# Latent scan of a gated DeltaNet: q products and intra-chunk products on the crossed quarters of the array

## The chip, the cores and the metric

The kernel runs on one core of a Trainium2 chip. The metric is the device time of one execution in microseconds (us). Three executions of the kernel before took 929.50, 930.94 and 931.32 us; their median is 930.94 us.

## The reference

One layer of a diffusion backbone: 512 latent tokens and 256 context tokens of width 1024. After modulation and RMSNorm one projection feeds two mixers, a windowed attention and a bidirectional gated DeltaNet; their outputs are projected, gated, summed, projected again and added to the stream, and an MLP follows. The change lies in the DeltaNet, which works in chunks of 64 tokens, for 8 heads of width 64 and two directions. A scan carries a 64 x 64 state per head from chunk to chunk:

```python
def step(S, xs):
    w_c, uv_c, qd_c, intra_c, kt_c, gl_c = xs
    u = uv_c - jnp.einsum('bhck,bhkv->bhcv', w_c, S)
    o = jnp.einsum('bhck,bhkv->bhcv', qd_c, S) + jnp.einsum('bhij,bhjv->bhiv', intra_c, u)
    S = jnp.exp(gl_c)[..., None, None] * S + jnp.einsum('bhck,bhcv->bhkv', kt_c, u)
    return S, o
```

The context scan (4 chunks) starts from zero and gives only its final states; these start the latent scans (8 chunks), forward and backward. The outputs of both directions are added, then normalized per head, scaled by `dn_norm_g` and multiplied by silu of a gate projection.

## The kernel before

Everything is in one program for one core. TensorE does the projections in three products each (high and low halves of both operands, in the fp32r type); the small products of the DeltaNet are plain float32. The compiler's planner orders each engine's instructions by its own estimates of when they are ready, and, among the ready ones, in the order in which the program writes them; it also places all semaphores. So the written order is a priority and not the order on the engine.

The heads lie in pairs: head pair q (0 to 3) has one head on partitions 0 to 63 and the other on 64 to 127. `r2` holds the two halves. A product on one half is a 64 x 64 product: its row half is where its two operands lie, its column half is where the result lies in PSUM.

`chain_step(d, step)` is one step of one direction, in three parts that are run in turn for both directions (`steps`). Part one multiplies the state with k and, in the latent scan, with q (L1116), and makes R from the k product on VectorE (L1120, L1121). Part two makes u (L1128), copies it scaled for the state (`uk`, VectorE, L1134) and plain for the output (`us`, ScalarE, L1138), and scales the q product into `zq` (ScalarE, L1140, one activation for each head pair, as the scale is one value per partition). Part three makes the next state: products of the k chunk with `uk` (L1147), the decayed old state (ScalarE, L1156), their difference (VectorE, L1158). Then the output: products of the intra-chunk matrices `IA` with `us` (L1165), added to `zq` (L1170); the direction that comes second to a chunk adds to the first one's result (L1173, L1175) and takes the sum of squares (L1176, L1177).

Each direction has two PSUM banks `zb[d]` for good: columns 0 to 255 hold the k products, 256 to 511 the q products, 512 to 767 u, 768 to 1023 the next state's products. The intra-chunk products get a bank of their own (`oi`).

Between the parts the loop at L1259 writes other work: `run_fill` with 8, 7 and 3 products of the gate projections (L1004, 128 x 128 by 512 columns), and `run_late`, which takes one piece of the late modulation (a 512 KB weight load, L1068, and a VectorE product with sum, L1070). The weights of the gate projections come through the same four buffers (L250) and are split into halves on ScalarE and VectorE (L259, L262). SP issues all loads.

After the scan the outputs are scaled (L1280), transposed (L1285) and multiplied by the gate's silu (L1290), where `a` picks the head of a pair.

Of the kernel before, what the change touches and what calls it, by code (L numbers as in the profile page):

```python
# [8 lines left out]
F32 = mybir.dt.float32  # L9
F32R = mybir.dt.float32r  # L10
BF16 = mybir.dt.bfloat16
AF = mybir.ActivationFunctionType
# [24 lines left out]
P = 128  # L37
# [5 lines left out]
HD = 64  # L43
NH = 8
CH = 64
# [54 lines left out]
def tile_layer(ctx: ExitStack, tc: tile.TileContext, I: dict, out: bass.AP, dbg=None):  # L100
    nc = tc.nc
    V, A, G, PE = nc.vector, nc.scalar, nc.gpsimd, nc.tensor
# [3 lines left out]
    const = ctx.enter_context(tc.tile_pool(name="const", bufs=1))  # L106
# [4 lines left out]
    def nm(s):  # L111
        uid[0] += 1
        return f"{s}_{uid[0]}"
# [5 lines left out]
    def small(shape, name, dt=F32, bufs=4, tag=None):  # L119
        return sb.tile(shape, dt, tag=tag or name, bufs=bufs, name=nm(name))  # L120

    alloc, bank = mem.get, lambda n=1: banks.get(n * 512)
# [60 lines left out]
    def split(src, hi, lo, eng=None):  # L183
        A.activation(r32(hi), src, AF.Copy)  # L184
        (eng or V).tensor_tensor(r32(lo), src, hi, op=ALU.subtract)  # L185
# [150 lines left out]
    for kt in range(KT):  # L336
        t = alloc(512)
        o = kt * 1024
# [316 lines left out]
    kT = [alloc(TOK, True) for _ in range(4)]  # L655
# [6 lines left out]
    t, t2 = alloc(TOK), alloc(TOK)  # L662
    ad, mx, be = t[0:32], t2[0:32], gb[32:64]
    for src, cols in ((abx, slice(0, SEQ)), (abc, slice(SEQ, TOK))):
        n = cols.stop - cols.start
# [27 lines left out]
    def col(c):  # L693

        return SEQ + c * CH if c < NCC else (c - NCC) * CH


    NM = NC_ * 4
# [16 lines left out]
    eG, tb, tbO = eg[:, 0:2], eg[:, 2:4], eg[:, 4]  # L715
# [180 lines left out]
    KTM, VTM = [None] * 3, [None] * 3  # L896
    qT = []
# [97 lines left out]
    szt, gdt = [], []  # L995
# [97 lines left out]
            next(fill, None)  # L1093


    oss = small([P, NCL, 4], "oss", bufs=1)
    hv = lambda ap: ap.rearrange("p (q v) -> p q v", q=4)
    state = [None, None]
# [3 lines left out]
    def chain_step(d, step):  # L1102
        lat = step >= NCC
        c = step if d == 0 else NC_ - 1 - (step - NCC) if lat else NCC - 1 - step
        cl = c - NCC if lat else c
        S, last = state[d], step == NC_ - 1
        m4 = slice(c * 4, c * 4 + 4)
        z = zb[d]
        r2 = [slice(0, 64), slice(64, 128)]
        vt = VTM[c // 4][:, c % 4 * 256:(c % 4 + 1) * 256]  # L1110

        if S is not None:
            for x, src in enumerate((kT, qT) if lat else (kT,)):
                for q in range(4):
                    for r in r2:
                        PE.matmul(z[r, x * 256 + q * HD:x * 256 + (q + 1) * HD], src[q][r, col(c):col(c) + CH],  # L1116
                                  S[r, q * HD:(q + 1) * HD], start=True, stop=True)
            Rb = alloc(256)
            R = Rb.ap
            V.tensor_tensor(hv(R), hv(z[:, 0:256]), bc(eG[:, d, m4], HD), op=ALU.mult)  # L1120
            V.scalar_tensor_tensor(R, vt, -0.5, R, op0=ALU.mult, op1=ALU.add)  # L1121
        else:
            R = vt
        yield
        u = z[:, 512:768]
        for q in range(4):
            for r in r2:
                PE.matmul(u[r, q * HD:(q + 1) * HD], XA[lat][d][r, (cl * 4 + q) * CH:(cl * 4 + q + 1) * CH],  # L1128
                          R[r, q * HD:(q + 1) * HD], start=True, stop=True)
        if S is not None:  # L1130
            Rb.free()
        if not last:
            uk = alloc(256)
            V.tensor_tensor(hv(uk.ap), hv(u), bc(tb[:, d, m4], HD), op=ALU.mult)  # L1134
        if lat:
            us, zqb = alloc(256), alloc(256)
            zq = zqb.ap
            A.activation(us.ap, u, AF.Copy)  # L1138
            for q in range(4):
                A.activation(zq[:, q * HD:(q + 1) * HD], z[:, 256 + q * HD:256 + (q + 1) * HD], AF.Copy,  # L1140
                             scale=eG[:, d, c * 4 + q:c * 4 + q + 1])
        yield
        if not last:
            sn = z[:, 768:1024]
            for q in range(4):
                for r in r2:
                    PE.matmul(sn[r, q * HD:(q + 1) * HD], KTM[c // 4][r, (c % 4 * 4 + q) * HD:(c % 4 * 4 + q + 1) * HD],  # L1147
                              uk[r, q * HD:(q + 1) * HD], start=True, stop=True)
            uk.free()
            Sn = Sb[d][step % 2]  # L1150
            if S is None:
                V.tensor_scalar(Sn.ap, sn, 0.5, None, op0=ALU.mult)
            else:
                se = alloc(256)
                for q in range(4):
                    A.activation(se[:, q * HD:(q + 1) * HD], S[:, q * HD:(q + 1) * HD], AF.Copy,  # L1156
                                 scale=egl[:, d, c * 4 + q:c * 4 + q + 1])
                V.tensor_tensor(Sn.ap, se.ap, sn, op=ALU.subtract)  # L1158
                se.free()
            state[d] = Sn  # L1160
        if lat:
            oi = bank()
            for q in range(4):
                for r in r2:
                    PE.matmul(oi[r, q * HD:(q + 1) * HD], IA[d][r, (cl * 4 + q) * CH:(cl * 4 + q + 1) * CH],  # L1165
                              us[r, q * HD:(q + 1) * HD], start=True, stop=True)
            us.free()
            dst = ot_[:, cl * 256:(cl + 1) * 256]
            if step - NCC < NCL // 2:
                V.tensor_tensor(dst, zq, oi[:, :256], op=ALU.add)  # L1170
                oi.free()
            else:
                V.tensor_tensor(zq, zq, oi[:, :256], op=ALU.add)  # L1173
                oi.free()
                V.tensor_tensor(dst, dst, zq, op=ALU.add)  # L1175
                A.activation(zq, dst, AF.Square)  # L1176
                V.tensor_reduce(oss[:, cl], hv(zq), axis=AX.X, op=ALU.add)  # L1177
            zqb.free()

    def steps(r):  # L1180
        for step in r:
            both = [chain_step(d, step) for d in range(2)]
            for _ in range(3):
                for g in both:
                    next(g, None)
                yield
# [42 lines left out]
    IA = [alloc(2048, True), alloc(2048, True)]  # L1229
# [39 lines left out]
    gdnh = small([P, 1], "gdnh", bufs=1)  # L1269
# [12 lines left out]
    for qq in range(2):  # L1282
        pt = bank(2)
        for c in range(NCL):
            PE.transpose(pt[:, c * P:(c + 1) * P], on[:, c * 256 + qq * P:c * 256 + (qq + 1) * P], ident)  # L1285
        for a in range(2):
            n = 2 * qq + a
            t = alloc(512)
            ct = lambda ap: ap.rearrange("p (c t) -> p c t", t=CH)
            V.scalar_tensor_tensor(ct(t.ap), pt.ap.rearrange("p (c a t) -> p c a t", a=2, t=CH)[:, :, a], gdnh, ct(szt[n].ap),  # L1290
                                   op0=ALU.mult, op1=ALU.mult)
            split(t.ap, yd[n][:, :512], yd[n][:, 512:])
            t.free()
            szt[n].free()
        pt.free()
# [106 lines left out]
    for hf in range(4):  # L1402
        act_ = []
        for f in range(FT):
# [7 lines left out]
            r, hl = alloc(1024), alloc(1024)  # L1412
# [135 lines left out]
```

## Time and profile before

| what | value |
|---|---|
| median of three runs | 930.94 us |
| profiled execution | 929.72 us |
| its span, first to last instruction | 927.7 us |
| granted TensorE clock, mean | 0.994 |
| TensorE busy | 894.8 us (96%) |
| VectorE busy | 597.7 us (64%) |
| ScalarE busy | 447.6 us (48%) |
| POOL busy | 12.1 us (1%) |
| latent scan, from its second k and q products to its last output products | 410.4 to 478.9 us |

The profile is one execution. PE is TensorE's products, PEld its weight loads, which overlap them, DVE VectorE, ACT ScalarE, POOL GpSimd, SP the queue that issues loads. A float32 product and its weight load stand in the trace as two records each. TensorE's products are pipelined and their ends are modelled, so their start times say more than their busy time. A row of a wait names who waited, for whom, how long in all, how often and how long at most. "m" stands for any buffer of the common arena, "banks" for PSUM.

### The profile page before, as it was taken

What the parts mean: (1) busy time and instruction counts of PE and PEld (TensorE: products, weight loads), DVE (VectorE), ACT (ScalarE), POOL (GpSimd) and SP (SyncE); (2) the same over time, 40 slices, a digit from 0 to 9 for tenths busy, and PEclk for the clock granted to TensorE, in tenths of its full rate; (3) what the DMA queues carried; (4) which work ended last, traced back from release to release, by engine and by line L of the source; (5) the groups of instructions that cost most, each with busy time, mean ns of one, the idle gap of its engine ahead of it and who ended that gap; (6) DMA issues with size and microseconds to landing.
All of it is one profiled execution on the core that took longest, in us unless ns stands there. A gap on an engine that the chain in (4) does not pass through costs nothing.

```text
span 927.7 us, 16848 instructions
## 1 busy us (share of the span) xinstructions
PE 894.8 (96%) x7082; PEld 721.1 (78%) x7082; DVE 597.7 (64%) x1021; ACT 447.6 (48%) x827; POOL 12.1 (1%) x26
## 2 busy tenths in 40 slices
PE   8999998999899999899999999999999999999998
PEld 5668767867677687778878879988888888888886
DVE  3587898997787997458756977971555235424511
ACT  5577753267568786565554434560243025213400
POOL 0000000000000002000000000000000000000000
PEclk9999998999999999999999999999999999999999
DMA  9650112210001232335424673680444224222111
GB/s 356 260 186 1 47 47 68 57 51 17 17 13 35 61 101 93 93 111 169 134 72 146 193 236 127 181 273 23 155 121 133 56 74 144 93 70 88 46 46 45
DMA packets 28443, 98.24 MB, mean 106 GB/s; under 512 B 3536, under 2 KB 4176, under 8 KB 27344
## 3 DMA queue, kind: packets, MB, share of 16 engines
q1 hardware_dynamic: 28368, 97.18, 32.7%
q8 instruction: 55, 0.90, 0.4%
q14 instruction: 20, 0.16, 0.1%
HBM read 95.07 MB, written 2.10 MB: 105 GB/s over the span
## 4 chain that ended last, share of the span: by engine, by line
PE 77%; DVE 11%; ACT 6%; DMA 3%; issue 2%; SPq 0%; DVEq 0%; ACTq 0%
PE banks L313 17%; PE banks L315 16%; PE banks L314 16%; PE banks L1004 10%; PE banks L1049 2%; PE banks L1116 2%; DVE wl L262 2%; PE banks L571 1%; PE banks L1147 1%; DMA wa<-in_wada 1%; PE banks L1128 1%; PE banks L577 1%; PE banks L639 1%; DVE m L834 1%; DVE m L833 1%
## 5 line engine op out<-in xcount | busy, mean ns | idle before, releaser
L313 PE MATMUL banks<-m,m 128*128 128x512 f32 (+1 forms) x600 | 223.3, 377 | 2.7 <-DVE m L620 1.9
L314 PE MATMUL banks<-m,m 128*128 128x512 f32 (+1 forms) x600 | 224.6, 376 | 0.1
L315 PE MATMUL banks<-m,m 128*128 128x512 f32 (+1 forms) x600 | 224.4, 376 | 0.0
L259 ACT ACTIVATE m<-wr 128x1024 fp32r<-128x1024 f32 x68 | 71.9, 1058 | 159.0 <-PE banks L314 80.4
L313 PEld LDWEIGHTS banks<-m,m 128*128 128x128 f32 x600 | 111.8, 188 | 25.8 <-ACT m L319 2.5
L314 PEld LDWEIGHTS banks<-m,m 128*128 128x128 f32 x600 | 112.5, 188 | 22.0 <-DVE m L320 1.5
L262 DVE TENSOR_TENSOR m<-wr,m 128x1024 fp32r<-128x1024 f32 x68 | 83.1, 1224 | 71.7 <-ACT m L259 35.4
L315 PEld LDWEIGHTS banks<-m,m 128*128 128x128 f32 x600 | 112.5, 188 | 21.4 <-issue 1.2
L1004 PE MATMUL banks<-m,wh 128*128 128x512 f32 x320 | 103.6, 400 | 3.0 <-ACT m L148 1.9
L315 PE MATMUL banks<-m,wl 128*128 128x512 f32 (+1 forms) x280 | 101.6, 365 | 4.7 <-DVE wl L262 4.7
L313 PE MATMUL banks<-m,wh 128*128 128x512 f32 (+1 forms) x280 | 104.0, 372 | 1.8 <-DVE m L595 1.0
L314 PE MATMUL banks<-m,wh 128*128 128x512 f32 (+1 forms) x280 | 102.8, 367 | 0.0
L1432 DVE SCALAR_TENSOR_TENSOR m<-banks,modT,m 128x512 f32<-128x512 f32 x32 | 24.0, 750 | 101.0 <-PE banks L315 101.0
L262 DVE TENSOR_TENSOR wl<-wr,wh 128x1024 fp32r<-128x1024 f32 (+1 forms) x58 | 62.1, 1071 | 28.6 <-ACT wh L259 28.5
L259 ACT ACTIVATE wh<-wr 128x1024 fp32r<-128x1024 f32 (+1 forms) x58 | 54.5, 940 | 41.7 <-PE banks L314 18.8
L1004 PEld LDWEIGHTS banks<-m,wh 128*128 128x128 f32 x320 | 58.9, 188 | 15.6 <-ACT m L148 2.2
L1004 PE MATMUL banks<-m,wl 128*128 128x512 f32 x160 | 64.7, 404 | 0.0
L315 PEld LDWEIGHTS banks<-m,wl 128*128 128x128 f32 x280 | 54.2, 195 | 12.8 <-DVE wl L262 5.4
L313 PEld LDWEIGHTS banks<-m,wh 128*128 128x128 f32 x280 | 54.4, 194 | 10.2 <-DVE m L595 1.3
L184 ACT ACTIVATE m<-m 128x512 fp32r<-128x512 f32 (+1 forms) x56 | 35.2, 631 | 54.5 <-DVE m L1415 21.3
L314 PEld LDWEIGHTS banks<-m,wh 128*128 128x128 f32 x280 | 54.4, 194 | 7.6 <-issue 1.0
L185 DVE TENSOR_TENSOR m<-m,m 128x512 fp32r<-128x512 f32 (+1 forms) x56 | 38.3, 688 | 18.8 <-ACT m L184 18.3
(236 smaller groups left out, 1279.2 us busy)
## 6 DMA issues: line engine op xcount, KB each, us to landing
wr<-in_wm SPq DMA_DIRECT2D x64, 512.0 KB, 3.7
wr<-in_win SPq DMA_DIRECT2D x38, 512.0 KB, 3.6
wa<-in_wada SPq DMA_DIRECT2D x32, 512.0 KB, 3.8
m<-in_wada SPq DMA_DIRECT2D x8, 1024.0 KB, 12.8
m<-in_xT SPq DMA_DIRECT2D x8, 512.0 KB, 5.7
wr<-in_wbr SPq DMA_DIRECT2D x16, 256.0 KB, 2.6
wr<-in_wout SPq DMA_DIRECT2D x8, 512.0 KB, 4.4
out<-m SPq DMA_DIRECT2D x8, 256.0 KB, 2.0
```

Source lines behind the costliest of these rows:

```text
L184: A.activation(r32(hi), src, AF.Copy)
L185: (eng or V).tensor_tensor(r32(lo), src, hi, op=ALU.subtract)
L259: h = A.activation(r32(hi), raw, AF.Copy)
L262: V.tensor_tensor(r32(lo), raw, hi, op=ALU.subtract)
L313: PE.matmul(acc, w[0][:, k, :], xhi, start=(start and i == 0), stop=False)
L314: PE.matmul(acc, w[0][:, k, :], xlo, start=False, stop=False)
L315: PE.matmul(acc, w[1][:, k, :], xhi, start=False, stop=(stop and i == n - 1))
L571: PE.transpose(pt[:, j * P:(j + 1) * P], probs[j][:, i * P:(i + 1) * P], ident)
L1004: PE.matmul(acc.ap, w[x][:, k, :], hx[k][y], start=(k == p == 0), stop=(k == KT - 1 and p == 2))
L1049: PE.matmul(pa.ap, w[x][:, j, :], r32(Q[y][:, :, j, :]), start=(j == p == 0), stop=(j == 3 and p == 2))
L1116: PE.matmul(z[r, x * 256 + q * HD:x * 256 + (q + 1) * HD], src[q][r, col(c):col(c) + CH], S[r, q * HD:(q + 1) * HD], start=True, stop=True)
L1432: V.scalar_tensor_tensor(xn_[ct], acc.ap, modT[:, 3, ct:ct + 1], xn_[ct], op0=ALU.mult, op1=ALU.add)
```

## The change

In the latent scan the q products are written to the other half of the partitions: the head on partitions 0 to 63 gets its q product on 64 to 127 and the other way round. The same holds for the intra-chunk products, so that both still meet in the sum; the output then holds the two heads of each pair exchanged, and the last hunk takes `1 - a` for `a`. The q products are written in turn with the k products, head pair by head pair, and the intra-chunk products in turn with those of the next state. In the banks of a direction q moves to columns 512 to 767 and u to 256 to 511, so k and u share one bank, and q and the next state's products the other. The scale of `zq` needs its halves exchanged too: `eGs` is a copy of `eG` with the halves swapped, made once by two ScalarE copies before the scans. The bank `oi` is taken before the next state's products instead of after them.

```diff
+    eGs = const.tile([P, 2, NM], F32, name="eGs")
+    for r in range(2):
+        A.activation(eGs[64 * r:64 * r + 64], eG[64 * (1 - r):64 * (1 - r) + 64], AF.Copy)
...
-            for x, src in enumerate((kT, qT) if lat else (kT,)):
-                for q in range(4):
-                    for r in r2:
-                        PE.matmul(z[r, x * 256 + q * HD:x * 256 + (q + 1) * HD], src[q][r, col(c):col(c) + CH],
+            for q in range(4):
+                for x, src in enumerate((kT, qT) if lat else (kT,)):
+                    for i, r in enumerate(r2):
+                        PE.matmul(z[r2[i ^ x], x * 512 + q * HD:x * 512 + (q + 1) * HD], src[q][r, col(c):col(c) + CH],
                                   S[r, q * HD:(q + 1) * HD], start=True, stop=True)
...
-        u = z[:, 512:768]
+        u = z[:, 256:512]
...
-                A.activation(zq[:, q * HD:(q + 1) * HD], z[:, 256 + q * HD:256 + (q + 1) * HD], AF.Copy,
-                             scale=eG[:, d, c * 4 + q:c * 4 + q + 1])
+                A.activation(zq[:, q * HD:(q + 1) * HD], z[:, 512 + q * HD:512 + (q + 1) * HD], AF.Copy,
+                             scale=eGs[:, d, c * 4 + q:c * 4 + q + 1])
         yield
+        sn = z[:, 768:1024]
+        oi = bank() if lat else None
+        for q in range(4):
+            o = slice(q * HD, (q + 1) * HD)
+            for r in r2:
+                if not last:
+                    PE.matmul(sn[r, o], KTM[c // 4][r, (c % 4 * 4 + q) * HD:(c % 4 * 4 + q + 1) * HD],
+                              uk[r, o], start=True, stop=True)
+            for i, r in enumerate(r2):
+                if lat:
+                    PE.matmul(oi[r2[1 - i], o], IA[d][r, (cl * 4 + q) * CH:(cl * 4 + q + 1) * CH],
+                              us[r, o], start=True, stop=True)
         if not last:
-            sn = z[:, 768:1024]
-            for q in range(4):
-                for r in r2:
-                    PE.matmul(sn[r, q * HD:(q + 1) * HD], KTM[c // 4][r, (c % 4 * 4 + q) * HD:(c % 4 * 4 + q + 1) * HD],
-                              uk[r, q * HD:(q + 1) * HD], start=True, stop=True)
             uk.free()
...
         if lat:
-            oi = bank()
-            for q in range(4):
-                for r in r2:
-                    PE.matmul(oi[r, q * HD:(q + 1) * HD], IA[d][r, (cl * 4 + q) * CH:(cl * 4 + q + 1) * CH],
-                              us[r, q * HD:(q + 1) * HD], start=True, stop=True)
             us.free()
...
-            V.scalar_tensor_tensor(ct(t.ap), pt.ap.rearrange("p (c a t) -> p c a t", a=2, t=CH)[:, :, a], gdnh, ct(szt[n].ap),
+            V.scalar_tensor_tensor(ct(t.ap), pt.ap.rearrange("p (c a t) -> p c a t", a=2, t=CH)[:, :, 1 - a], gdnh, ct(szt[n].ap),
```

## The prediction

> **What bounds the kernel now.** I read the head of the page first, then the table of stretches over the latent scan, then the chain that ended last, then the waits.
>
> ```profile
> span 927.7 us, 16848 instructions
> PE 894.8 (96%) x7082; PEld 721.1 (78%) x7082; DVE 597.7 (64%) x1021; ACT 447.6 (48%) x827; POOL 12.1 (1%) x26
> ```
>
> TensorE is busy for 96% of the span, but its ends are modelled, so this alone proves nothing about one stage. The changed lines run in the latent scan, whose steps 1 to 7 I cut at the start of their k and q products (columns: stretch, its length, then busy us with instruction counts of PE, PEld, DVE, ACT and POOL, granted clock, DMA share, GB/s):
>
> ```profile
> 410.40:420.30 9.90, 9.90 (x181) 8.09 (x182) 7.31 (x15) 5.51 (x23) 0.00 (x0) 1.00 0.35 108
> 420.30:430.10 9.80, 9.80 (x179) 7.97 (x179) 7.87 (x18) 4.69 (x16) 0.00 (x0) 1.00 0.56 163
> 430.10:440.90 10.80, 10.37 (x181) 8.27 (x180) 9.56 (x21) 6.72 (x24) 0.00 (x0) 1.00 0.72 209
> 440.90:450.80 9.90, 9.90 (x181) 8.09 (x182) 7.69 (x20) 6.30 (x22) 0.00 (x0) 1.00 0.66 201
> 450.80:460.70 9.90, 9.90 (x181) 8.07 (x183) 8.13 (x20) 4.31 (x16) 0.00 (x0) 1.00 0.36 100
> 460.70:470.50 9.80, 9.80 (x180) 7.97 (x180) 6.72 (x16) 6.13 (x21) 0.00 (x0) 1.00 0.19 66
> 470.50:478.90 8.40, 8.40 (x145) 6.73 (x144) 4.99 (x17) 4.67 (x14) 0.00 (x0) 1.00 0.31 96
> ```
>
> A step takes 9.8 to 9.9 us, all of it TensorE; only the step at 430 is longer. VectorE is next with 6.7 to 9.6 us. The chain through one step (start, length, work, instructions) is TensorE without a break:
>
> ```profile
> 440.93 2.01 PE banks L1116 x64
> 442.94 2.04 PE banks L1004 x8
> 444.98 1.08 PE banks L1128 x32
> 446.06 1.81 PE banks L1004 x7
> 447.88 0.61 PE banks L1147 x16
> 448.49 0.47 PE banks L1165 x16
> 448.95 0.47 PE banks L1147 x16
> 449.42 0.47 PE banks L1165 x16
> 449.89 0.90 PE banks L1004 x3
> ```
>
> A float32 product stands as two records, so 64 records at L1116 are the 32 products of both directions. TensorE itself waited twice in the whole scan, 1.5 us in all:
>
> ```profile
> PE banks L1004 <- ACT wh L259: 1.1, 1, 1.1
> PE banks L1147 <- ACT m L1138: 0.4, 1, 0.4
> ```
>
> So here the sum of the TensorE pieces is the time, and what shortens L1116, L1147 and L1165 shortens the step, until VectorE is in the way.
>
> **The change part by part: the products.** Before, the two products of one head pair use two quarters of the array (lower rows to lower columns, upper to upper). L1165 has 16 records in 0.47 us: eight pairs, 59 ns a pair. After, four products that use four different quarters stand next to each other. No row of before has the two crossed quarters together with the straight ones, so I bound the price of a group of four. The nearest rows are these (start, length, operation, shape, count):
>
> ```profile
> 76.51 1.57 PE L704 MATMUL banks<-c_prm,m 64*64 64x16 f32 x48
> 381.74 1.10 PE L754 MATMUL banks<-m,m 64*32 64x64 f32 x64 [0.19 <-ACT m L148]
> L704 PE MATMUL banks<-c_prm,m 64*64 64x16 f32 x48 | 1.6, 207 | 0.0
> L754 PE MATMUL banks<-m,m 64*32 64x64 f32 x256 | 4.2, 217 | 0.2 <-ACT m L148 0.2
> ```
>
> L704 has the same 64 rows feed both column halves, one product after the other: (1.57 - 0.21) / 24 = 57 ns a pair, though only 16 columns stream, so it is the loading of the 64 weight columns that takes this time, and two loads from one row half pass at once. L754 has each row half feed two column groups, with 64 columns streaming: (1.10 - 0.22) / 16 = 55 ns for four records, not for two. So one row half can feed two places at once, in weights and in data, and four records can run in the time of two. Not shown is that two row halves write the same column half at once, and both loads at full width in all four quarters. The ends: 59 ns for four (all overlap) and 118 ns for four (they take turns, no gain). I take 59, since L754 is the nearest: same streaming length, same number of records in flight.
>
> Per stage 32 pairs become 16 groups, 16 x 0.059 = 0.94 us less: L1116 from 2.01 to 1.07, the four rows of L1147 and L1165 from 2.02 to 1.08. L1128 stays. The latent scan has eight k and q stages and seven with both L1147 and L1165 (the last step has no next state). The first k and q stage isn't on the path; the planner has put it ahead, at 388 to 392 us, where the path is ScalarE's copies of the intra-chunk matrices:
>
> ```profile
> 398.80 0.63 ACT m L1249
> 399.66 1.33 ACT m L1140 x6
> 401.99 5.99 PE banks L1004 x25
> ```
>
> So 14 stages count: 14 x 0.94 = 13.2 us off TensorE's path.
>
> By the Trainium skill, page TensorE: Matmul & The Clock Gate, Part 3, The mechanism, a weight load runs under a product in flight only where the row group differs. By that rule the crossed pair, which shares its rows with the straight one, would load behind it, and the saving would be near zero. The trace doesn't agree so far: at L754 two tiles share each row half and still four records pass in 55 ns.
>
> **VectorE takes part of it back.** In the seven stretches VectorE's busy time is 7.31 + 7.87 + 9.56 + 7.69 + 8.13 + 6.72 + 4.99 = 52.3 of 68.5 us, and the change removes none of it. Its two longest waits are these (total, times, longest):
>
> ```profile
> DVE m L1158 <- PE banks L1147: 5.2, 4, 2.1
> DVE m L1070 <- DMA wa<-in_wada: 3.5, 4, 1.2
> ```
>
> The wait on TensorE shrinks with it; the 3.5 us on weights for the late modulation don't. VectorE takes its queue in order, so what waits behind L1070 are L1120, L1121, L1134 and L1158, and TensorE waits for these. I put the longer of the two engines for each stretch. TensorE: the stretch less 1.88 (the last less 0.94). VectorE: its busy time plus its DMA waits where the timeline has them:
>
> ```profile
> 428.05 1.23 DVE L1070 SCALAR_TENSOR_TENSOR m<-wa,m 128x1024 f32<-128x1024 f32 x1 [1.15 <-DMA wa<-in_wada]
> 435.76 1.22 DVE L1070 SCALAR_TENSOR_TENSOR m<-wa,m 128x1024 f32<-128x1024 f32 x1 [1.20 <-DMA wa<-in_wada]
> 445.53 1.23 DVE L1070 SCALAR_TENSOR_TENSOR m<-wa,m 128x1024 f32<-128x1024 f32 x1 [0.78 <-DMA wa<-in_wada]
> ```
>
> That gives 8.02; 7.87 + 1.15 = 9.02; 9.56 + 1.20 = 10.76; 7.69 + 0.78 = 8.47; 8.13; 7.92; 7.46. The sum is 59.8, where TensorE alone needs 68.5 - 13 x 0.94 = 56.3. So 3.5 us are lost again, nearly all in the steps at 420 and 430, where L1070 is dense. The bounds: 0 (VectorE works ahead in the lighter steps) and 7 (the same again for stalls inside a step, where a product waits for L1121 or L1138 while the step as a whole has room).
>
> **Waits that move.** Two waits of before are between readers and writers of different columns of the same PSUM bank:
>
> ```profile
> ACT m L1140 <- DVE m L1120: 7.3, 6, 2.1
> PEld banks L1147 <- ACT m L1138: 2.0, 4, 0.9
> 444.39 0.93 ACT L1140 ACTIVATE m<-banks,eg 128x64 f32<-128x64 f32 x4 [0.88 <-DVE m L1120]
> ```
>
> L1140 needs nothing from L1120, and L1147 nothing from L1138; what they share is the bank, so the program orders accesses by bank. After, k and u share one bank, q and the next state the other. L1140 no longer waits for L1120, which is worth nothing, as ScalarE isn't the path. The next state's products now wait for L1140 (through the bank) where they waited for L1138, and behind them in TensorE's queue stand the fill products L1004 and the next step's L1116. In the step shown, the second L1140 ends at 445.3 and L1147 starts at 447.8: 2.5 us of cover, of which TensorE's shorter first stage takes 0.94. Cost 0; without that cover 0.93 us for four scalings a direction. The products with us (L1165) now stand between the state's own, so the state waits for L1138 too, as it already did through the bank.
>
> **Small parts.** The two added copies for the swapped scales run once before the scans, 64 x 96 elements each. Between these rows,
>
> ```profile
> L1156 ACT ACTIVATE m<-m,egl 128x64 f32<-128x64 f32 x44 | 11.7, 339 | 5.8 <-DVE m L1158 5.7
> L1247 ACT ACTIVATE m<-m 32x512 f32<-32x512 f32 x1 | 0.6, 630 | 0.0
> ```
>
> one takes 0.34 to 0.63 us, two at most 0.8 by the nearer row with its extra columns. Their source is ready long before, so they fit into ScalarE's earlier gaps: 0, or 0.8 if they fall where ScalarE sets the path. The swapped half at L1290 and the other scale tile cost nothing: same operations, counts and shapes. No DMA is added or moved, and SP's and POOL's queues are as before.
>
> **Sum.** 13.2 - 3.5 - about 0.3 for the copies and lost order = 9.4 us. Against the profiled execution, 929.72 us (span 927.7 and 2.0 around it), that is 920.3; the median of the three runs, 930.94, is 1.2 above it, so 921.5.
>
> **The rivals.**
> 1. The whole saving arrives. For it: VectorE's longest wait is on TensorE, and the planner may set L1070 elsewhere. Against: the DMA waits. 930.94 - 13.2 = 917.7; chance 0.13.
> 2. The planner takes state and output products apart. One step of before shows that it does this where it thinks the copy of u late:
>
> ```profile
> 437.80 0.68 PE L1147 MATMUL banks<-m,m 64*64 64x64 f32 x16 [0.43 <-ACT m L1138]
> 438.84 0.68 PE L1147 MATMUL banks<-m,m 64*64 64x64 f32 x16
> 439.36 1.15 PE L1165 MATMUL banks<-m,m 64*64 64x64 f32 x32
> ```
>
> Both L1147 run ahead of both L1165. Were it so in every step, only the seven k and q stages gain: 6.6, less 1 for VectorE: 925.3. Chance 0.14, with VectorE at the far end of its bounds.
> 3. The change doesn't do what it says: the crossed products take turns with the straight ones, 118 ns for four. L1116 to L1165 keep their times: 930.9. Against it is L754; for it, that no row shows two row halves on one column half. Chance 0.08.
> 4. Slower: where two row halves write the same columns, the array has to empty between them. An emptying has a price in the chain above: L1147 after L1004 takes 0.61, L1165 right after L1147 0.47, so 0.14 a change. With a change between straight and crossed pairs, 16 in a direction's stage, 32 in a stage: 14 x 32 x 0.14 = 63 us, so 994. It decides as soon as a change costs anything over the zero of rival 3. Neither L704 nor L754 shows a pause between tiles of one row half. Chance 0.07, in which I count unlikelier ways of the same sign.
>
> **How the numbers follow.** My forecast, 918.5 to 924.5, has 0.58; rival 1 has 0.13, rival 2 0.14, rival 3 0.08, rival 4 0.07. A measurement of this kernel can tell about 0.2%, 1.9 us. Faster: 0.58 + 0.13 + 0.14 = 0.85; same 0.08; slower 0.07. The range goes from 916.5 (rival 1 with 1.2 us less, as the profiled run lies below the median) to 927 (past rival 2, with VectorE's 7 us): it leaves out rivals 3 and 4.
>
> **What would show it.** Right: 64 records of the k and q stage in about 1.1 us, the mixed stage of both directions in 1.1, steps of 8 to 8.5 us, VectorE over 85% busy in them, and new TensorE waits on L1121, L1138 or L1158 around the dense L1070. Wrong in the products: the stage still at 2.0 us. Wrong in the cover: TensorE waiting for L1140. The forecast fails low if the steps at 420 and 430 shrink like the others, and high if state products run alone.

## The result

| kernel | median, us | executions | ratio to the kernel before, 95% interval |
|---|---|---|---|
| before | 931.15 | 20 | |
| after | 926.64 (923.26 to 929.45) | 20 | 0.9953 [0.9939, 0.9966] |

The kernel is 4.5 us faster where 9.4 us were forecast. The time lies in the forecast's range and the sign is right, but less than half of the gain came: the forecast was wrong in its size. The step that failed is the term for VectorE. The profiled execution of after took 923.26 us, 6.5 less than that of before, and is the quickest of its twenty; the difference between single executions is taken up at the end.

The head of the page of after, the two lines that answer to the first two of before:

```profile
span 921.5 us, 16859 instructions
PE 886.7 (96%) x7082; PEld 709.2 (77%) x7082; DVE 596.6 (65%) x1021; ACT 447.6 (49%) x829; POOL 12.0 (1%) x26
```

VectorE and ScalarE have the work they had; ScalarE's two new instructions are the copies for the swapped scales. The timeline of TensorE in after (start, length, line, shape, count of records) shows the k and q products, then the first and last rows of a mixed stage:

```profile
410.68 1.16 PE L1119 MATMUL banks<-m,m 64*64 64x64 f32 x64
411.77 0.50 PE L1004 MATMUL banks<-m,wl 128*128 128x512 f32 x1
...
425.24 0.27 PE L1152 MATMUL banks<-m,m 64*64 64x64 f32 x2
425.29 0.27 PE L1156 MATMUL banks<-m,m 64*64 64x64 f32 x2
...
426.37 0.50 PE L1004 MATMUL banks<-m,wl 128*128 128x512 f32 x1
```

(L1119 was L1116, L1152 was L1147, L1156 was L1165.) The k and q products take 411.77 - 410.68 = 1.09 us to the next instruction, where 1.07 was forecast and 2.01 stood before. The mixed stage takes 426.37 - 425.24 = 1.13. Now the steps, cut as for before at the start of their k and q products (length, then busy us of PE, PEld, DVE, ACT and POOL, clock, DMA share, GB/s):

```profile
410.70:418.80 8.10, 8.10 (x183) 6.21 (x182) 6.49 (x16) 4.64 (x19) 0.00 (x0) 1.00 0.45 134
418.80:427.70 8.90, 8.44 (x183) 6.35 (x182) 7.99 (x17) 5.14 (x19) 0.00 (x0) 1.00 0.62 180
427.70:438.20 10.50, 9.41 (x178) 6.98 (x178) 9.81 (x24) 6.63 (x24) 0.00 (x0) 1.00 0.73 208
438.20:446.70 8.50, 8.50 (x180) 6.47 (x179) 7.14 (x17) 5.10 (x20) 0.00 (x0) 1.00 0.66 215
446.70:455.90 9.20, 8.11 (x181) 6.21 (x180) 7.83 (x19) 4.88 (x19) 0.00 (x0) 1.00 0.28 92
455.90:465.40 9.50, 8.47 (x179) 6.49 (x178) 6.91 (x17) 6.44 (x22) 0.00 (x0) 1.00 0.35 106
465.40:473.30 7.90, 7.24 (x143) 5.73 (x143) 6.41 (x16) 4.78 (x14) 0.00 (x0) 1.00 0.37 102
sum 62.60, PE 58.27 PEld 44.43 DVE 52.58 ACT 37.61 POOL 0.00; mean PE 8.32 PEld 6.35 DVE 7.51 ACT 5.37 POOL 0.00
```

| step | 1 | 2 | 3 | 4 | 5 | 6 | 7 | sum |
|---|---|---|---|---|---|---|---|---|
| forecast | 8.02 | 9.02 | 10.76 | 8.47 | 8.13 | 7.92 | 7.46 | 59.8 |
| after | 8.1 | 8.9 | 10.5 | 8.5 | 9.2 | 9.5 | 7.9 | 62.6 |

Step 7 is cut here, and in all sums over a scan below, where its last output product starts; that of before was cut where it ends, so the 68.5 us of before are 0.2 us longer by their cut. In this execution steps 1 to 4 go as forecast, to 0.3 us. Steps 5 to 7 take 26.6 instead of 23.5 us, and in none of them is an engine busy all the time: at step 6 TensorE has 8.47 of 9.5 us and VectorE 6.91. TensorE's longest waits over this scan (us in all, times, longest):

```profile
PE banks L1131 <- DVE m L1124: 1.9, 2, 1.1
PE banks L1119 <- DVE m L1168: 1.0, 2, 0.7
PE banks L1152 <- DVE m L1137: 0.9, 1, 0.9
```

Each is a small VectorE operation of the recurrence. Step 5 shows why it is late. VectorE's timeline there, and the product that waits:

```profile
448.04 0.68 DVE L626 SCALAR_TENSOR_TENSOR m<-m,banks 128x512 f32<-128x512 f32 x1
448.64 1.22 DVE L262 TENSOR_TENSOR wl<-wr,wh 128x1024 fp32r<-128x1024 f32 x1
449.78 0.41 DVE L1182 TENSOR_REDUCE oss<-m 128x4 f32<-128x256 f32 x1
450.11 0.74 DVE L1123 TENSOR_TENSOR m<-banks,eg 128x256 f32<-128x256 f32 x2
450.77 0.75 DVE L1124 SCALAR_TENSOR_TENSOR m<-m,m 128x256 f32<-128x256 f32 x2
...
451.24 1.15 PE L1131 MATMUL banks<-m,m 64*64 64x64 f32 x32 [1.09 <-DVE m L1124]
```

The k products started at 446.7 and were done about 1.1 us later. VectorE then still had the gate's output L626, the split of the fill weights L262 and a sum of squares (L1182) ahead of L1123. From 448.0 us on it works without a pause: nothing was missing for these, they only stood first in its queue. Between this stage and u the program writes eight fill products, 2.04 us in the chain of before. Before, the stage itself took 2.01 us, so VectorE had 0.94 us more to come through its queue. The same step of before shows that it needed nearly all of it:

```profile
451.79 1.22 DVE L262 TENSOR_TENSOR wl<-wr,wh 128x1024 fp32r<-128x1024 f32 x1
453.92 0.75 DVE L1121 SCALAR_TENSOR_TENSOR m<-m,m 128x256 f32<-128x256 f32 x2
454.77 1.15 PE L1128 MATMUL banks<-m,m 64*64 64x64 f32 x32
```

The queue is the same, L626 and L262 ahead of L1120 and L1121 (L1123 and L1124 of after). L1121 ends at 453.92 + 0.75 = 454.67, and L1128 starts at 454.77: 0.1 us to spare, where the change takes 0.94 away. In step 6 of after the same thing happens a part later, behind ScalarE:

```profile
460.61 1.23 DVE L262 TENSOR_TENSOR wl<-wr,wh 128x1024 fp32r<-128x1024 f32 x1 [1.28 <-ACT wh L259]
461.76 0.68 DVE L626 SCALAR_TENSOR_TENSOR m<-m,banks 128x512 f32<-128x512 f32 x1
462.35 0.74 DVE L1137 TENSOR_TENSOR m<-banks,eg 128x256 f32<-128x256 f32 x2
...
462.92 0.41 PE L1152 MATMUL banks<-m,m 64*64 64x64 f32 x6 [0.91 <-DVE m L1137]
```

VectorE stands idle for 1.28 us at L262 until ScalarE has made the high half, and L1137, which the next state needs, stands behind it.

### The profile page after: what moved, and what is told of

It reads as the page before. It is cut to its first block, busy times and chain, and to the rows that moved or that the text cites. A ratio compares the mean times of both kernels' runs of the same rounds, so it can differ in the third digit from the quotient of the medians.

```text
span 921.5 us, 16859 instructions
## 1 busy us (share of the span) xinstructions
PE 886.7 (96%) x7082; PEld 709.2 (77%) x7082; DVE 596.6 (65%) x1021; ACT 447.6 (49%) x829; POOL 12.0 (1%) x26
## 4 chain that ended last, share of the span: by engine, by line
PE 45%; DVE 3%; DMA 3%; ACT 1%; issue 1%; ACTq 0%
PE banks L313 14%; PE banks L314 14%; PE banks L315 14%; PE banks L1004 3%; DMA wa<-in_wada 2%; DVE m L1070 1%; DVE wl L262 1%; DMA wr<-in_wm 0%; ACT wh L259 0%; DVE m L1168 0%; ACT m L1166 0%; PE banks L1131 0%; PE banks L1290 0%; PE banks L1156 0%; ACT m L148 0%
## 5 line engine op out<-in xcount | busy, mean ns | idle before, releaser
L262 DVE TENSOR_TENSOR m<-wr,m 128x1024 fp32r<-128x1024 f32 x68 | 83.1, 1224 | 69.9 <-PE banks L314 34.2
L262 DVE TENSOR_TENSOR wl<-wr,wh 128x1024 fp32r<-128x1024 f32 (+1 forms) x58 | 62.1, 1071 | 29.7 <-ACT wh L259 29.3
```

Source lines behind the costliest of these rows:

```text
L262: V.tensor_tensor(r32(lo), raw, hi, op=ALU.subtract)
```

## The experiments

All times are medians, and the kernels are told in the order in which they ran, four at a time; before, run beside them, had 930.31, 931.5, 930.97 and 930.39 us for the four groups. "Scan" is the sum of the seven steps, as in the table above. The theory at the start was the forecast's: TensorE's saving is whole, and VectorE, held by the late modulation, takes part of it back.

**One part of the change at a time.** The first kernel keeps the crossed quarters and writes the products in the old order:

```diff
-            for q in range(4):
-                for x, src in enumerate((kT, qT) if lat else (kT,)):
+            for x, src in enumerate((kT, qT) if lat else (kT,)):
+                for q in range(4):
...
+        if lat:
+            oi = bank()
+            for q in range(4):
+                o = slice(q * HD, (q + 1) * HD)
+                for i, r in enumerate(r2):
+                    PE.matmul(oi[r2[1 - i], o], IA[d][r, (cl * 4 + q) * CH:(cl * 4 + q + 1) * CH],
+                              us[r, o], start=True, stop=True)
```

> The changed kernel with its crossed quarters, its bank layout and its scale copy, but with the products in the old order: all k, then all q; all of the next state, then the intra-chunk ones. Theory A (the gain comes from four quarters at once, and the rest of the change costs nothing): k and q stage 2.0 us again, state and output stage 2.0, time of the kernel before within 1 us. Rival B (the new bank layout or the new plan costs something by itself): 1 to 4 us slower than before, with waits on L1143 or a worse order in the scan.

928.71 us, 0.9987 [0.9975, 0.9999], scan 67.6. The stage did not go back to 2.0 us. TensorE's timeline of this kernel, where the program now has all L1151 of a direction ahead of its L1171:

```profile
413.00 1.56 PE L1119 MATMUL banks<-m,m 64*64 64x64 f32 x64
414.49 0.50 PE L1004 MATMUL banks<-m,wl 128*128 128x512 f32 x1
...
419.45 0.51 PE L1151 MATMUL banks<-m,m 64*64 64x64 f32 x10
419.75 0.27 PE L1171 MATMUL banks<-m,m 64*64 64x64 f32 x2
419.79 0.28 PE L1151 MATMUL banks<-m,m 64*64 64x64 f32 x3
```

The stage takes 414.49 - 413.00 = 1.49 us, between the 1.09 of the written turns and the 2.01 of before. Of the 16 records of the first direction's L1151 only ten have started when L1171, written behind all of them, starts on the other two quarters. The planner didn't mix them: in TensorE's instructions as this kernel compiles, the 16 records of L1151 stand together and the 16 of L1171 behind them. So TensorE starts products ahead of their order when their quarter is free, but only a little ahead; writing them in turn gives the other 0.4 us. The Trainium skill, page TensorE: Matmul & The Clock Gate, Part 3, The mechanism, says that products start and end in strict order; for the starts, these rows do not agree.

The next two kernels put the old order back in one of the two places only (the k and q products in turn; the mixed stage in turn).

> Only the k and q products in turn; next state first and then intra-chunk as before. TensorE loses 7 x 0.92 = 6.4 us in the scan. Theory A (VectorE's queue takes back what goes past its own need): 3 to 5 us faster than before, so most of what the whole change gave (4.3 us). Rival C (each stage's saving arrives in the same share, about a third): 2 us faster.

> Only the next state's and the intra-chunk products in turn; k first and then q. TensorE loses 7 x 0.92 = 6.4 us. Theory A: 3 to 5 us faster than before. Rival C: 2 us faster. The two halves of the change adding to more than the whole (4.3 us) speaks for A, to just the whole for C.

927.62, 0.9969 [0.9957, 0.9981], scan 65.3, and 925.74, 0.9959 [0.9942, 0.9976], scan 63.9. Both stages have their sizes where nothing holds them up, 1.09 in turn and 1.49 not, so against the old order the k and q stages give 7 x 0.4 = 2.8 us on TensorE and the mixed ones 6 x 0.4 = 2.4. The old order itself takes 13 x 0.52 = 6.8 us off TensorE against before, and its scan is only 0.9 us shorter: something else has become the limit. Whether the savings of the two halves add up can't be told. They gain 930.31 - 927.62 = 2.7 and 930.31 - 925.74 = 4.6 us over before, the old order 1.6 and the whole change 4.5, with intervals that reach 1.1 to 1.6 us to either side; the theories of these two runs stay undecided.

**The late modulation.** All sixteen late pieces are written ahead of the scan, in after and in before:

```diff
-        if n % 3:
-            run_late(LATE)
...
         run_fill(FILL[1] - CPAUSE)
+        run_late(4)
...
         run_fill(FILL[2] - FPAUSE)
+        run_late(4)
```

> The changed kernel with the 16 pieces of the late modulation (load and L1070) written before the latent scan, four in each of the four rounds that make the triangular and intra-chunk matrices, and none in the scan. Theory A (VectorE's queue with L1070 holds the scan back): the scan from its second k and q stage to its last output products falls from 62.8 to about 57 us, TensorE's waits on L1124, L1137 and L1168 mostly go, and the kernel is 8 to 11 us faster than before. Rival D (the state's own chain through VectorE and ScalarE is as long as a shortened step): the scan stays at 61 to 63 us and the kernel 4 to 5 us faster than before. Where the pieces cost time before the scan, the scan shows the theory and the total doesn't.

> The kernel before with the 16 pieces of the late modulation moved ahead of the latent scan in the same way. Theory A: TensorE bounds the scan, so only the 1 us lost in the step at 430 goes: scan 67 to 68 us against 68.5, 0 to 1.5 us faster than before. Rival D: the same. If it is 4 us or more faster, what the move gives has nothing to do with the change.

928.26, 0.998 [0.9967, 0.9993], and 935.96, 1.0048 [1.0032, 1.0065]. The scan of after falls to 59.2 us, that of before only from 68.5 to 67.5: before, the late pieces cost next to nothing in the scan, as TensorE covered them; with the change they cost 3.4 us (5.5 by the second execution of after, below). But they are work wherever they stand: the scan starts at 418.6 instead of 410.7. And steps 5 and 6 do not move. Their two rows of the table of stretches, and then TensorE's waits in them:

```profile
452.40:461.60 9.20, 8.11 (x179) 6.21 (x178) 6.83 (x18) 5.51 (x22) 0.00 (x0) 1.00 0.22 61
461.60:470.80 9.20, 8.46 (x179) 6.42 (x178) 7.10 (x18) 5.79 (x21) 0.00 (x0) 1.00 0.10 31
```

```profile
PE banks L1131 <- DVE m L1124: 1.1, 1, 1.1
PE banks L1152 <- DVE m L1137: 0.7, 1, 0.7
```

These are the waits of after at the same places, with not one L1070 in the steps. The part of the theory that blames the late modulation holds for steps 2 to 4 and falls for 5 and 6.

What of L1070 slows steps 2 to 4, VectorE's time or the loads? Two kernels take one away each: L1070 over 128 of its 1024 columns with its loads (and the same in before), and L1070 at full width on a buffer that lies there, without loads.

```diff
-            V.scalar_tensor_tensor(t.ap, wa, 0.5, scr.ap, op0=ALU.mult, op1=ALU.mult, accum_out=modT[:, grp, j:j + 1])
+            V.scalar_tensor_tensor(t[:, :128], wa[:, :128], 0.5, scr[:, :128], op0=ALU.mult, op1=ALU.mult, accum_out=modT[:, grp, j:j + 1])
```

```diff
-            wa = sb.tile([P, KT, P], F32, tag="wr", bufs=NWR, name=nm("wa")).rearrange("p k c -> p (k c)")
-            nc.sync.dma_start(out=wa, in_=I["wada2"][grp, j])
+            wa = scr.ap
```

> The changed kernel with L1070 over 128 of its 1024 columns; all loads and their waits stay. It leaves out seven eighths of the sums that make the late modulation. This splits VectorE's own time from the lateness of the loads. Theory A1 (VectorE's time in L1070): scan from 62.8 to 57 to 59 us, 7 to 10 us faster than before. Theory A2 (the loads land late and hold the queue): scan stays at 61 us or more, 4 to 6 us faster than before.

> The kernel before with L1070 over 128 of its 1024 columns, all loads kept; it leaves out the same seven eighths. A control for the run beside it: theory A says 0 to 1.5 us faster than before, since TensorE bounds the scan; what it gains beyond that lies outside the scan.

> The changed kernel again, on the same chip as the three beside it: 3.5 to 5.5 us faster than before by the first result; scan 62 to 64 us.

> The changed kernel with L1070 at full width but without its loads: it multiplies a buffer that is there already, so the sums of the late modulation are wrong. With the run that kept the loads and cut the product (scan 63.3 us, no shorter) this tells VectorE's time from the lateness of the loads. Theory A2 (loads that land late hold VectorE's queue): scan 58 to 60 us, steps 2 to 4 at 8.0 to 8.7, steps 5 and 6 still above 9. Theory A1 (VectorE's time): scan stays at 62 us or more.

Short products: 922.26, 0.9906 [0.9886, 0.9925], scan 63.3 (before with them 927.56, 0.9952 [0.9933, 0.9971], 69.0). No loads: 922.63, 0.9915 [0.9888, 0.9942], scan 61.9. After again: 927.63, 0.9953 [0.9935, 0.9971], scan 64.7, more than the 62 to 64 expected, in steps of 8.1, 10.1, 10.9, 9.0, 9.2, 9.5 and 7.9. So two executions of one kernel differ by 2.1 us in the scan, all of it in steps 2 to 4, and smaller differences between two kernels there say little; steps 5 and 6 are the same in both. Neither kernel frees the scan, for different reasons. VectorE's wait in the kernel with short products, and step 3 of the kernel without loads:

```profile
DVE m L1070 <- DMA wa<-in_wada: 7.0, 4, 3.8
```

```profile
427.50:437.90 10.40, 9.93 (x179) 7.11 (x179) 10.40 (x24) 6.50 (x23) 0.00 (x0) 1.00 0.09 33
```

With short products VectorE is through early and waits for the loads, 7.0 us where after waits 2.6, with the recurrence behind it. Without loads VectorE is busy for the whole 10.40 us. Time and loads stand in for each other: steps 2 to 4 together take 29.5 us with short products and 27.1 without loads, 27.9 and 30.0 in the two executions of after, and only without both, as with early pieces, 25.5. Both kernels are faster all the same, but so is before with short products, by 931.5 - 927.56 = 3.9 us with its scan no shorter: that gain lies outside the scan, and where wasn't followed.

**VectorE's work to GpSimd.** The split L262 of the scan goes to GpSimd, then the output addition L1180 too, then both with early pieces:

```diff
-        V.tensor_tensor(r32(lo), raw, hi, op=ALU.subtract)
+        (G if onpool[0] else V).tensor_tensor(r32(lo), raw, hi, op=ALU.subtract)
...
-                V.tensor_tensor(dst, dst, zq, op=ALU.add)
+                G.tensor_tensor(dst, dst, zq, op=ALU.add)
```

> The changed kernel with the split of the gate weights that is written in the scan (L262 there) on GpSimd instead of VectorE. Theory E (in steps 5 and 6 VectorE takes L626 and L262 ahead of L1123, so u is late by 1.2 us): the step that lost it falls from 9.2 to 8.0 to 8.3 us. Rival D (the state's own chain is as long as the shortened step): steps 5 and 6 stay at 9.2 and 9.5. If GpSimd's split is so slow that the gate products wait for it, the stalls move to L1004 and the run decides nothing.

> As the run before it, and the second direction's addition to the output (L1180) on GpSimd too. Theory E: steps 5 to 7 fall to about 8.0 to 8.3 each, the scan by 1.5 to 3 us against the changed kernel; steps 2 to 4, where loads hold VectorE, stay. Rival D: no step falls by more than 0.3 us.

> Late modulation ahead of the scan, split and output addition on GpSimd: all three suspects gone at once. Theory A2 with E: scan 56 to 57 us, as TensorE's own 56.3 us, every step 8.0 to 8.3. Rival D: 59 us as with the late modulation moved alone. The total holds the cost of the moved pieces before the scan (4.5 us in the kernel before), so it is 4 to 6 us faster than before at most.

931.9, 1.0007 [0.9989, 1.0025], scan 68.6; 935.7, 1.0043 [1.0026, 1.006], scan 74.7; 928.8, 0.9978 [0.9963, 0.9994], scan 60.3. With the late pieces in the scan the gain is gone, and with early pieces the scan is longer than the 59.2 us without GpSimd, where 56 to 57 was expected. (The 74.7 can't be set beside the others: that profiled execution, 941.13 us, is the slowest of its twelve, and four of its steps have a granted clock of 0.79 to 0.90. Two steps of the 68.6 have 0.96 and 0.87.) From the first of these kernels, the splits as a group (busy us and mean ns after the bar), then rows of the timeline:

```profile
L262 POOL TENSOR_TENSOR wl<-wr,wh 128x1024 fp32r<-128x1024 f32 x6 | 14.8, 2466 | 67.8 <-ACT wh L259 42.5 <-DVE m L1169 12.9 <-PE banks L1005 12.3
```

```profile
411.21 2.40 POOL L262 TENSOR_TENSOR wl<-wr,wh 128x1024 fp32r<-128x1024 f32 x1 [12.95 <-DVE m L1169]
411.64 2.51 DVE L1010 SCALAR_TENSOR_TENSOR m<-m,m 128x512 f32<-128x512 f32 x1 [0.31 <-ACT m L148]
...
416.02 1.48 PE L1132 MATMUL banks<-m,m 64*64 64x64 f32 x32 [1.89 <-DVE m L1125]
```

The split takes 2466 ns on GpSimd against 1220 on VectorE, but no fill product of the scan waits for it. It is VectorE that pays. L1010 (L1009 of after, 0.68 us there) starts during a split and ends about 0.5 us after it, having taken 2.51 us, and behind it and one L1071 TensorE waits 1.89 us for L1125 (L1124 of after). Two more operations within the scan's steps do the same: one L1071 takes 2.78 us instead of 1.22, one L1181 1.55 instead of 0.42. Others that start during a split, such as L1169 with an operand in PSUM, keep their 0.41 us. So the kernels trade one long operation in VectorE's queue for another, and settle nothing about who held VectorE's order before.

**The split taken away.** What was open: is it VectorE's order in steps 5 and 6, or simply the latency of the chain k product, scaling, u, scaling, state? Inside the scan the split is left out, alone and together with early pieces:

```diff
+        if inscan[0]:
+            return r32(hi), r32(hi)
         V.tensor_tensor(r32(lo), raw, hi, op=ALU.subtract)
         return r32(hi), r32(lo)
```

> The kernel after, but inside the latent scan the subtraction that makes the low half of the fill weights (L262, six of 128x1024, 1.22 us each on VectorE) is left out and the fill products take the high half in its place: no product is dropped, the gate values are wrong. Theory (steps 5 and 6 of the scan are set by what stands ahead of the scalings L1123, L1124 and L1137 in VectorE's fixed order, L262 above all): the two steps of 9.2 and 9.5 us fall to 8.1 to 8.6, the scan from 62.6 to 60 or 61, the time to about 924.5. Rival (they are set by the latency of the chain k product, scaling, u, scaling, state, whatever else VectorE does): 9.2 and 9.5 stay, the scan loses less than 0.7 us, the time stays near 927.

> As the run before this one (no L262 in the latent scan), and all 16 late modulation pieces written ahead of the scan as in the run with early pieces, where the scan took 59.2 us with steps of 9.2 and 9.2 us left. Theory: with both large VectorE operations gone TensorE is the bound again, every step takes 7.9 to 8.3 us, the scan 56 to 57.5 us (the forecast's TensorE term alone was 56.3). Rival (latency of the chain): steps 5 and 6 stay above 9, the scan at 58.5 to 59.5. The time itself: the early pieces cost some 8 us before the scan, so 925 to 928.

925.71, 0.9947 [0.9927, 0.9967], scan 62.6; and 925.15, 0.9939 [0.9918, 0.996], scan 55.9. Steps 5 to 7 of the second kernel, and the sum of all seven:

```profile
449.40:457.80 8.40, 8.29 (x181) 6.26 (x180) 5.83 (x16) 6.28 (x24) 0.00 (x0) 1.00 0.21 66
457.80:465.80 8.00, 8.00 (x179) 6.20 (x178) 5.82 (x17) 5.73 (x20) 0.00 (x0) 1.00 0.12 36
465.80:472.80 7.00, 7.00 (x143) 5.63 (x143) 3.27 (x10) 4.79 (x14) 0.00 (x0) 1.00 0.01 2
sum 55.90, PE 55.78 PEld 43.27 DVE 32.43 ACT 37.55 POOL 0.00; mean PE 7.97 PEld 6.18 DVE 4.63 ACT 5.36 POOL 0.00
```

TensorE is busy for 55.78 of 55.90 us, each of the six full steps takes 8.0 to 8.4, and the rival falls: the chain's own latency fits into a step of 8 us. The forecast's TensorE term was 56.3. So the whole saving is there once the two long VectorE operations, and the loads of one of them, are out of the way, and these are what takes 62.6 - 55.9 = 6.7 us back. (The time gains little by it, since the early pieces start the scan at 416.9 instead of 410.7.) The split alone, though, did not give what was expected. With it gone, the planner dealt VectorE's queue anew, and in step 5 the late modulation took its place. The stretch, and then rows of its timeline:

```profile
448.50:458.70 10.20, 8.72 (x179) 6.54 (x178) 7.58 (x20) 6.03 (x20) 0.00 (x0) 1.00 0.31 89
```

```profile
455.19 1.23 DVE L1073 SCALAR_TENSOR_TENSOR m<-wa,m 128x1024 f32<-128x1024 f32 x1 [1.27 <-DMA wa<-in_wada]
...
456.82 0.33 PE L1155 MATMUL banks<-m,m 64*64 64x64 f32 x4 [0.45 <-DVE m L1140]
```

L1073 is L1070 of after, L1140 its L1137, L1155 its L1152. VectorE waits 1.27 us for a load and then works 1.23, and the second direction's scaling, due long before, stands behind it. Step 6 of the same kernel fell from 9.5 to 8.1. So the theory holds as "whatever long operation stands ahead of the scalings", not as "the split". In its step 5 the k and q products also stood still for 0.9 us, for which the profile names no releaser; that stays open.

**The fill dealt anew.** Two kernels that compute the same as after: 10, 6 and 2 fill products between the parts in place of 8, 7 and 3, and 42 instead of 36 ahead of each half of the intra-chunk matrices.

```diff
-FILL = 144, 28, 36, (8, 7, 3)
+FILL = 144, 28, 36, (10, 6, 2)
```

```diff
-FILL = 144, 28, 36, (8, 7, 3)
+FILL = 144, 28, 42, (8, 7, 3)
```

> The kernel after with the 18 fill products of a step dealt 10, 6 and 2 in place of 8, 7 and 3: two more stand between the k and q products and u, where L1124 was late, one less between u and the state, one less after it. The output is the reference's. Theory (the order on VectorE): the cover moves 0.5 us to the place of the longest wait and leaves two others with less, so the scan changes by at most 1 us either way and the time by less than 1.5 us. Rival (the wait for L1124 at u is the whole of the lost time): scan 60 to 61, time 924.5 to 925.

> The kernel after with 42 in place of 36 fill products before each half of the intra-chunk matrices, so that 12 products move from after the scan to ahead of it and the gate tiles' split (L259, L262) and its output (L626) fall into other parts of the scan's steps. The output is the reference's. Theory (the fixed order of VectorE's queue sets steps 5 and 6): the steps of 9.2 and 9.5 us change their places or sizes, the sum of the scan stays within 1.5 us of 62.6, the time within 1.5 us of 927. Rival (latency of the chain): steps 5 and 6 stay 9.2 and 9.5 as in every kernel so far.

928.53, 0.9977 [0.9961, 0.9993], scan 66.5; 924.61, 0.9936 [0.9914, 0.9958], scan 62.9. Moving cover to the longest wait costs more elsewhere: the rival there (one wait is all) falls, and the theory's bound of 1 us was too small. With the shift the steps are 9.7, 9.5, 8.1, 8.6, 9.6, 10.2 and 7.2. Steps 1 and 2 have become long and step 3 short, and the sum stays, as the theory has it; steps 5 and 6 change their sizes but stay long, so they speak less clearly than the kernel without both operations. The time misses the 927 of the expectation by more than its 1.5 us. It is the fastest of the kernels that compute the reference, 2 us below after, but the intervals overlap and the gain isn't in the scan, so no claim is made for it.

## Why the prediction was right in one term and wrong in another

**The products: right.** Four records in the time of two was the choice at 59 ns, from L754. The stages measure 1.09 and about 1.1 against 1.07 and 1.08, and TensorE's term for the seven stretches, 56.3, measured 55.9 (56.1 by before's cut) where nothing else is in the way. Rivals 3 (no overlap) and 4 (the array empties, 994) are out. The prediction's rule from the Trainium skill, page TensorE: Matmul & The Clock Gate, Part 3, The mechanism, by which the crossed pair loads behind the straight one of its rows, does not agree with the 1.09 us.

**VectorE: wrong, the term was mis-sized.** "So 3.5 us are lost again" is the step that failed. The stretches took 62.6 instead of 59.8 us, so VectorE took 62.6 - 55.9 = 6.7 back, and in the second execution of after 64.7 - 55.9 = 8.8. On TensorE's side, 62.6 - 58.27 = 4.3 us of the 6.7 are gaps; the rest are stages drawn out because their second half waits (in steps 2 and 3 L1131 takes 1.48 us, in step 1 1.15). The rule, the longer of two engines per stretch, gave steps 1 to 4 to 0.3 us in one execution; in the other, steps 2 to 4 took 30.0 where it gave 28.25, so this closeness is in part luck. It failed in 5 to 7, by 3.1 us, in both. It asks whether VectorE has room in a step, and in those steps it has: 6.91 of 9.5. It does not ask in which third of the step that room lies. The queue is in order, and L262, L626 or a waiting L1070 ahead of L1123, L1124 or L1137 holds up TensorE though the sum would fit. The prediction named this as the far end of its bound (0 to 7: "stalls inside a step") and took the middle; 6.7 is close to that end and 8.8 beyond it. The rows that would have told were in the profile of before: in its step 5 the scalings were done 0.1 us before L1128 needed them, in a stage that was to lose 0.94. Such cover was costed for L1147 behind L1140 but not for L1128 behind L1121.

**The start of the scan: counted, not earned.** The forecast counted 14 stages, one of them (the first mixed one, 0.94 us) ahead of the first stretch. There, the planner took the state's product alone:

```profile
402.39 0.68 PE L1152 MATMUL banks<-m,m 64*64 64x64 f32 x16
```

The scan starts at 410.7, before at 410.4: the 0.94 didn't come, and 0.3 were lost. In before's chain the path up to 401.99 us is ScalarE's; that it still is in after is argued, not shown. The state's product alone is rival 2 at one of its places. In the mixed stage shown above the two products go in turn, as they do in most others, so that rival 2's 925.3 is near the measured time is luck. Rival 1, the whole saving, needs the 55.9 us that only the kernel without both long operations has. From the forecast of 9.4 us go the 2.8 of the stretches and these 0.94 + 0.3 = 1.2; 0.6 that were gained behind the scan (448.8 to 448.2 us from its end to the end of the span) and the 0.3 set aside for the copies come back: 9.4 - 2.8 - 1.2 + 0.6 + 0.3 = 6.3. The profiled spans differ by 927.7 - 921.5 = 6.2. (The 0.2 us by which the cuts differ stand in the 2.8 and in the 0.6 and cancel.)

**Bank waits and copies: right.** In after the waits of TensorE's products have neither L1143 (L1140 of before) nor the copies, which take 0.28 us each and run long before the scans, at 86 to 88 us.

**Between the profiled pair and the medians** lie another 2 us. The second profiled execution of after had a span of 927.7 us, 6.2 more than the first. 4.1 of these lie ahead of the scan, which starts at 414.8 instead of 410.7. Stretches of the second execution there (the granted clock is the third number from the end), and one of the first:

```profile
380.00:390.00 10.00, 10.00 (x114) 7.67 (x116) 3.06 (x4) 4.59 (x12) 0.00 (x0) 0.88 0.35 105
...
400.00:410.00 10.00, 9.86 (x66) 7.72 (x65) 5.28 (x10) 7.89 (x22) 0.52 (x1) 0.86 0.23 63
```

```profile
400.00:410.00 10.00, 9.79 (x110) 7.53 (x110) 4.24 (x8) 6.08 (x18) 0.00 (x0) 1.00 0.46 149
```

The other 2.1 us lie in the scan, where the granted clock is 1.00 in every step of both. They are in steps 2 to 4, and VectorE waits longer for the loads of the late modulation, in the first execution and in the second:

```profile
DVE m L1070 <- DMA wa<-in_wada: 2.6, 4, 0.9
DVE m L1070 <- DMA wa<-in_wada: 4.6, 4, 2.1
```

The forecast took before's profiled execution, 1.2 us under its median, as the base, and the median of after lies 3.4 above its profiled one. So a part of the missing gain is the VectorE term again, which the first profile shows too small. That the clock makes the 4.1 us ahead of the scan is argued from these rows, not shown, and how the medians divide between clock and loads is open.

## What to carry to other kernels

Small products that use two quarters of the array leave the other two free; written in turn, with results crossed to the other half of the partitions, they cost next to nothing beside the first pair (64 records in 1.09 us, 32 on two quarters in 1.08). Before such a saving is credited, go through each in-order engine's queue between the shortened stage and the next one and ask which long operation stands ahead of the short one that the next stage needs: the sum of an engine's work per step says only that there is room, not that it lies in the right place. The time by which the short one was early before the change is what may be taken away (0.1 us here). Where either of two long operations (the late products and the weight split here) can stand in the same place, taking one away shows little; take away both. And before two scans are compared, profile one kernel twice: here that alone gave 2.1 us.

## What was not expected of the hardware

- TensorE starts products ahead of written order when their quarter is free, over a few products: 1.49 us for a stage that takes 2.01 on two quarters and 1.09 with the turns written out.
- Some VectorE operations with both operands in SBUF that start while GpSimd works on 128x1024 elements (2466 ns) end only after it: 2.51 instead of 0.68 us, 2.78 instead of 1.22, 1.55 instead of 0.42. Those with an operand in PSUM keep their time (0.41 us).
- The granted clock dips to 0.86 over 10 us in one execution of after and stays at 1.00 in another, in the same stretch ahead of the scan.
- At a granted clock of 1.00 two executions of one kernel differ by 2.1 us in the scan, with 2.0 us more of waits for loads.
